# Starting SBUF tiles at multiples of 512 bytes in a hybrid decoder layer

## The chip, the cores and the metric

One core of a Trainium2 chip runs the whole layer in one launch. The metric is device microseconds of one execution; the kernel before takes 1169.69 us, the median of 3 runs (1168.28 to 1171.7).

## What is computed

One layer of a decoder on x of 512 tokens by 1024, in float32. Cut to what matters:

```python
x = x + 0.5 * swiglu(rms_norm(x), w_gate, w_up, w_down)          # D_FF = 2816
h = rms_norm(x); z, xbc, dt, q, k, v = split(h @ w_in)
xs, b, c = split(silu(causal_dwconv(xbc)))
y = rms_norm(ssd_chunked(xs, softplus(dt), -exp(a_log), b, c) * silu(z))   # 16 heads, chunks of 128
o = rms_norm(diff_attention(rms_norm(q), rms_norm(k), v))                  # 8 heads, causal
x = x + concat[y, o] @ w_out
x = x + 0.5 * swiglu(rms_norm(x), w_gate2, w_up2, w_down2)
```

## The kernel before

`hymba_layer` keeps activations transposed, as 8 blocks of 128 channels by 512 tokens. Matrix products are done in three float32r passes: an operand is split into a high part `hi` (rounded to float32r) and the rest `lo`, and hi·hi, hi·lo and lo·hi are summed in PSUM. `mm3` (lines 153 to 157) is that triple for a 128x128 block of weights (`lhsT`, the stationary operand, loaded by an LDWEIGHTS of its own for each matmul) and 512 columns of activations (`rhs`, the moving operand):

```python
PE.matmul(ps, lhsT=hi, rhs=xh, start=start, stop=False)
PE.matmul(ps, lhsT=hi, rhs=xl, start=False, stop=False)
PE.matmul(ps, lhsT=lo, rhs=xh, start=False, stop=stop)
```

Weights stream from HBM into `raw` (three buffers, SP's queue, line 106), ACT casts them to `whi` (line 113) and DVE subtracts to get `wlo` (line 114), four buffers each, pieces ahead of their use.

The stages in order:

- FFN1. Its first 6 blocks of D_FF go the plain way: `gu` (`std`, line 359, through `mm3`), 8 blocks of 3 matmuls for each of gate and up, with `xh`, `xl` moving. The other 16 go pair by pair through a seven-product scheme (`seven`, line 314): `product` (lines 307 to 312) runs matmuls of 256 columns with slices of `ah`, `al` moving, into `s`. The down product `dn` (`down`, line 339, through `mm3`) has `h` moving, and line 346 adds it to `x`.
- The mixer's projections: `xbc` (12 blocks, through `mm3`, `xhm` and `xlm` moving, line 565), dt, then z and v (`tok_pair`, lines 619 to 621), where a 128x128 block of `xhm` or `xlm` is stationary and 512 columns of `whi` or `wlo` move, in two pieces of 256; and q and k (`tok_proj`, lines 596 to 598), with 256 columns of weights moving. SSD (from line 645) runs between the z and v pieces, attention (`att_s`, `att_t`, `att_av`, `att_o`) between the q and k pieces. SSD and attention use float32 matmuls, which the trace shows as two records each.
- `wo` (`y_part`, `o_part`, lines 917 to 930, through `mm3`), with `yh`, `yl` or `ov`, `ool` moving.
- FFN2, as FFN1, but with 4 plain blocks and 18 in pairs; its `xh`, `xl` come from the pool `x2` on the right side of SBUF.

Tiles come from pools that lie one behind the other in SBUF, and a tile's start in its partition is the sum of what lies before it. `const` comes first, then `wpool` (raw, whi, wlo), `tiny`, `xn` (`xh`, `xl`), and on top of these the pools of a stage; `x1` and `x2` grow from the other end (`side="right"`). A tile whose size is no multiple of 512 shifts all behind it: `const` holds small ones, `row` is 1456 float32 wide (line 412), `u` 515 (line 455).

Of the kernel before, what the change touches and what calls it, by code (L numbers as in the profile page):

```python
# [8 lines left out]
F32 = mybir.dt.float32  # L9
# [9 lines left out]
P = 128  # L19
T = 512  # L20
# [14 lines left out]
NROW = 1456  # L35
# [3 lines left out]
def hymba_layer(ctx: ExitStack, tc: tile.TileContext, xT, gu1, dn1, wxbc, wdt, wz, wv, wqk,  # L39
# [3 lines left out]

    const = ctx.enter_context(tc.tile_pool(name="const", bufs=1))
    wpool = ctx.enter_context(tc.tile_pool(name="wpool", bufs=4))
    dram = ctx.enter_context(tc.tile_pool(name="dram", bufs=1, space=DRAM))
    pspool = ctx.enter_context(tc.tile_pool(name="psum", bufs=8, space=PSUM))

# [137 lines left out]
    G.memset(epst, EPS)  # L186

    tiny = ctx.enter_context(tc.tile_pool(name="tiny", bufs=2))
    xn_cm = tc.tile_pool(name="xn", bufs=1)
    xnpool = xn_cm.__enter__()  # L190

# [217 lines left out]

    mix_cm = tc.tile_pool(name="mix", bufs=1)  # L410
    mix = mix_cm.__enter__()
    row = mix.tile([P, NROW], F32, name="row")
    nc.sync.dma_start(row, rows.partition_broadcast(P))
    vt = [mix.tile([P, NB, 256], F32, tag=f"v{g}", name=f"v{g}") for g in range(4)]

# [21 lines left out]
    ssd = ssd_cm.__enter__()  # L437
# [7 lines left out]
    ea = ssd.tile([P, NB, 16], F32, name="ea")  # L445
    dsd = ssd.tile([P, NB, 16], F32, name="dsd")
    cdec = ssd.tile([P, NB, 16], F32, name="cdec")
    acs_d = dram.tile([64, P], F32, name="acs_d")
    ysave = dram.tile([P, KD, NB, P], F32, name="ysave")

    cv_cm = tc.tile_pool(name="conv", bufs=2)
    cv = cv_cm.__enter__()

    def conv_tile(t, ps):
        u = cv.tile([P, T + 3], F32, tag="u", name="u")
        G.memset(u[:, 0:3], 0.0)
        V.tensor_mul(u[:, 3:], ps, nm.rbc)
        a = cv.tile([P, T], F32, tag="a", name="a")

        def cw(i):  # L460
            c = C_CW + t * 4 + i
            return col[:, c:c + 1]

        V.tensor_scalar(a, u[:, 3:], cw(3), col[:, C_CB + t:C_CB + t + 1], op0=ALU.mult, op1=ALU.add)
        for i in range(3):
            V.scalar_tensor_tensor(a, u[:, i:i + T], cw(i), a, op0=ALU.mult, op1=ALU.add)
        if t >= 8:
            dst = (bT if t < 10 else cT)[:, t % 2, :]
        else:
            dst = cv.tile([P, T], F32, tag="xst", name="xst")  # L470
        S.activation(dst, a, AF.Silu)
        return dst
# [75 lines left out]
    for n, pair in enumerate(order):  # L548
        if n == 2:
            pt_dt = dt_proj()  # L550
            small_consts()
        ps = [pP(f"xbc{n}{i}") for i in range(2)]
        if n == 0:
            ws = [piece(), piece()]
            for k in range(KD):
                for p_, w in zip(ps, ws):
                    mm3(p_, w, k, nm.xh[:, k, :], nm.xl[:, k, :], k == 0, k == KD - 1)
            fin = nm.finish()
            next(fin)
            first_ps = ps  # L560
            continue
        for i in range(2):
            w = piece()
            for k in range(KD):
                mm3(ps[i], w, k, nm.xh[:, k, :], nm.xl[:, k, :], k == 0, k == KD - 1)
            if n == 1 and i == 0:
                next(fin)
                pend0 = [(t, conv_tile(t, p_)) for t, p_ in zip(order[0], first_ps)]
        if n == 3:
            dt_finish(pt_dt)  # L570
        for t, dst in pend:
            conv_tr(t, dst)
        pend = [(t, conv_tile(t, ps[i])) for i, t in enumerate(pair)]
        if n == 1:
            pend = pend0 + pend
# [517 lines left out]
```

## Time and profile before

| | |
|---|---|
| median of 3 runs | 1169.69 us |
| the profiled execution, its own time | 1168.65 us |
| its span, first to last instruction | 1166.9 us |
| mean granted TensorE clock | 0.997 of 2.4 GHz |
| PE busy | 1158.3 us |
| DVE busy | 854.2 us |
| ACT busy | 543.5 us |
| DMA, mean rate | 102 GB/s |

PE's matmuls overlap each other in the trace: a matmul's record runs from its start to its modelled end, and the next starts before. The distance between the starts of two neighbours, called a step below, is read from the timeline.

### The profile page before, as it was taken

Reading aid. Unit: us, or ns where it says so; the run is one execution under the profiler, and the core shown is the slowest. Engines: PE = TensorE matmul, PEld = TensorE weight load, DVE = VectorE, ACT = ScalarE, POOL = GpSimd, SP = SyncE. Lnnn points to the kernel's source line nnn. Section 1 sums busy time; section 2 is a strip of 40 time slices with the busy share of each in tenths; the row PEclk is TensorE's granted clock in tenths of the full one; section 3 lists DMA queues with packets and bytes.
Section 4 is the critical chain, followed back from the end, with each engine's and each line's share of the span. In section 5 each row is a group of like instructions: output and inputs, shape, how many; then the busy total and the mean of one; then the engine's idle time right before and its main releaser. Section 6 shows DMA issues by size and latency. Waiting matters only on the chain.

```text
span 1166.9 us, 17871 instructions
## 1 busy us (share of the span) xinstructions
PE 1158.3 (99%) x7051; PEld 1004.0 (86%) x7051; DVE 854.2 (73%) x1501; ACT 543.5 (47%) x922; POOL 36.1 (3%) x63
## 2 busy tenths in 40 slices
PE   8999999999999999999999999999999999999998
PEld 6789999999887788788988887688889999999986
DVE  7877877877768975785477877435798888777763
ACT  5533343434345459784466656334354443334331
POOL 1000000000013000000000000022000000000000
PEclk9999999999999999999999999899999999999999
DMA  7223333433246242333321105054223333333332
GB/s 238 88 73 96 91 111 103 110 98 105 86 123 213 73 145 86 114 100 100 109 73 44 67 19 154 19 171 127 69 67 99 110 114 95 117 97 99 113 96 86
DMA packets 44692, 119.49 MB, mean 102 GB/s; under 512 B 4864, under 2 KB 10176, under 8 KB 44608
## 3 DMA queue, kind: packets, MB, share of 16 engines
q1 hardware_dynamic: 43328, 114.15, 32.3%
q0 software_dynamic: 1280, 4.20, 1.0%
q8 instruction: 55, 0.90, 0.3%
q14 instruction: 29, 0.24, 0.1%
HBM read 112.00 MB, written 6.32 MB: 101 GB/s over the span
## 4 chain that ended last, share of the span: by engine, by line
PE 99%; DVE 0%; DMA 0%; SPq 0%; ACT 0%; issue 0%
PE s L312 10%; PE s L310 10%; PE s L311 10%; PE dn L157 7%; PE dn L156 7%; PE dn L155 7%; PE gu L155 3%; PE gu L157 3%; PE gu L156 3%; PE qk L596 3%; PE wo L155 3%; PE wo L156 3%; PE wo L157 3%; PE qk L598 3%; PE qk L597 3%; PE sc L835 2%
## 5 line engine op out<-in xcount | busy, mean ns | idle before, releaser
L113 ACT CAST whi<-raw 128x1024 fp32r<-128x1024 f32 (+2 forms) x217 | 189.4, 875 | 312.8 <-PE s L311 124.1
L114 DVE TENSOR_TENSOR wlo<-raw,whi 128x1024 fp32r<-128x1024 f32 (+3 forms) x225 | 223.0, 993 | 129.2 <-ACT whi L113 122.1
L311 PE MATMUL s<-al,whi 128*128 128x256 f32 x952 | 266.4, 281 | 0.0
L310 PE MATMUL s<-ah,whi 128*128 128x256 f32 x952 | 265.4, 281 | 0.0
L312 PE MATMUL s<-ah,wlo 128*128 128x256 f32 x952 | 264.9, 281 | 0.0
L311 PEld LDWEIGHTS s<-al,whi 128*128 128x128 f32 x952 | 179.4, 188 | 2.2
L310 PEld LDWEIGHTS s<-ah,whi 128*128 128x128 f32 x952 | 178.8, 188 | 2.3
L312 PEld LDWEIGHTS s<-ah,wlo 128*128 128x128 f32 x952 | 178.3, 188 | 0.1
L156 PE MATMUL dn<-h,whi 128*128 128x512 f32 x352 | 139.0, 395 | 0.0
L157 PE MATMUL dn<-h,wlo 128*128 128x512 f32 x352 | 138.7, 395 | 0.0
L155 PE MATMUL dn<-h,whi 128*128 128x512 f32 x352 | 137.9, 395 | 0.0
L113 ACT CAST whi<-tw 128x1024 fp32r<-128x1024 f32 x68 | 70.3, 1050 | 143.0 <-PE s L311 68.9
L114 DVE TENSOR_TENSOR wlo<-tw,whi 128x1024 fp32r<-128x1024 f32 x68 | 81.9, 1218 | 2.9 <-ACT whi L113 2.9
L157 PEld LDWEIGHTS dn<-h,wlo 128*128 128x128 f32 x352 | 66.1, 188 | 15.0
L155 PEld LDWEIGHTS dn<-h,whi 128*128 128x128 f32 x352 | 66.0, 188 | 14.3
L156 PEld LDWEIGHTS dn<-h,whi 128*128 128x128 f32 x352 | 66.1, 188 | 13.9
L596 PE MATMUL qk<-whi,xhm 128*128 128x256 f32 x256 | 74.3, 290 | 0.0
L598 PE MATMUL qk<-whi,xlm 128*128 128x256 f32 x256 | 71.9, 281 | 0.0
L597 PE MATMUL qk<-wlo,xhm 128*128 128x256 f32 x256 | 71.5, 279 | 0.0
L346 DVE SCALAR_TENSOR_TENSOR x<-dn,x 128x512 f32<-128x512 f32 x64 | 44.0, 687 | 37.3 <-PE dn L157 36.7
L155 PE MATMUL gu<-xh,whi 128*128 128x512 f32 x160 | 64.2, 402 | 1.8 <-DVE acc L232 1.7
L157 PE MATMUL gu<-xh,wlo 128*128 128x512 f32 x160 | 62.9, 393 | 0.0
(274 smaller groups left out, 2101.2 us busy)
## 6 DMA issues: line engine op xcount, KB each, us to landing
raw<-in_gu SPq DMA_DIRECT2D x86, 512.0 KB, 3.7
raw<-in_dn SPq DMA_DIRECT2D x48, 384.0 KB, 3.2
raw<-in_wqk SPq DMA_DIRECT2D x16, 512.0 KB, 3.7
raw<-in_wxbc SPq DMA_DIRECT2D x12, 512.0 KB, 3.7
raw<-in_wo SPq DMA_DIRECT2D x10, 512.0 KB, 3.7
raw<-in_dn SPq DMA_DIRECT2D x16, 256.0 KB, 2.7
raw<-in_wz SPq DMA_DIRECT2D x16, 256.0 KB, 3.0
ab<-acs_d SPq DMA_DIRECT2D x8, 512.0 KB, 4.0
```

What stands on the lines that cost most here:

```text
L113: S.copy(hi[:, a:b], raw[:, a:b])
L114: V.tensor_sub(lo[:, a:b], raw[:, a:b], hi[:, a:b].bitcast(F32))
L155: PE.matmul(ps, lhsT=hi, rhs=xh, start=start, stop=False)
L156: PE.matmul(ps, lhsT=hi, rhs=xl, start=False, stop=False)
L157: PE.matmul(ps, lhsT=lo, rhs=xh, start=False, stop=stop)
L310: PE.matmul(ps, lhsT=hi, rhs=ah[:, i, a], start=i == 0, stop=False)
L311: PE.matmul(ps, lhsT=hi, rhs=al[:, i, a], start=False, stop=False)
L312: PE.matmul(ps, lhsT=lo, rhs=ah[:, i, a], start=False, stop=i == 3)
L346: V.scalar_tensor_tensor(x[d], ps, 0.5, x[d], op0=ALU.mult, op1=ALU.add)
L596: PE.matmul(o, lhsT=xh, rhs=hi, start=k == 0, stop=False)
L597: PE.matmul(o, lhsT=xh, rhs=lo, start=False, stop=False)
L598: PE.matmul(o, lhsT=xl, rhs=hi, start=False, stop=k == KD - 1)
```

## The change

It sets unused tiles and wider tiles between the others. `padc` adds 288 bytes to `const`, `padr` 480 to the right side, `padt` 32 to `tiny`, `pads` 192 to `ssd`; `row` grows from 5824 to 6144 bytes and `u` from 2060 to 2560, both used to their old width.

```diff
     wpool = ctx.enter_context(tc.tile_pool(name="wpool", bufs=4))
+    const.tile([P, 72], F32, name="padc")
+    rpad = ctx.enter_context(tc.tile_pool(name="rpad", bufs=1, side="right"))
+    rpad.tile([P, 120], F32, name="padr")
...
     tiny = ctx.enter_context(tc.tile_pool(name="tiny", bufs=2))
+    tiny.tile([P, 8], F32, tag="padt", name="padt", bufs=1)
...
-    row = mix.tile([P, NROW], F32, name="row")
+    row = mix.tile([P, 1536], F32, name="row")[:, :NROW]
...
     cdec = ssd.tile([P, NB, 16], F32, name="cdec")
+    ssd.tile([P, 48], F32, name="pads")
...
-        u = cv.tile([P, T + 3], F32, tag="u", name="u")
+        u = cv.tile([P, T + 128], F32, tag="u", name="u")[:, :T + 3]
```

z and v are projected onto 512 columns in both kernels. Each engine's instructions, their order and their waits are the same in both programs. What differs is where the tiles start; the two compiled programs place them so, in bytes past a multiple of 512 (every buffer of a name is alike):

| tile | before | after |
|---|---|---|
| `raw`, `whi`, `wlo` | 224 | 0 |
| `xh`, `xl` of FFN1, `xhm`, `xlm`, `yh`, `yl` | 192 | 0 |
| `ah`, `al`, `h`, `tx` | 192 | 0 |
| `x` (`x1`, `x2`), `xh`, `xl` of FFN2 | 480 | 0 |
| v, `ov`, `ool`, `qT`, `kT`, `pe`, `aT`, `on`, `xs`, `sz`, `bT`, `cT` | 384 | 0 |
| `ab`, `xdt`, `y` | 192 | 0 |
| `state` | 128 | 448 |
| `ident`, `identr` | 480 | 256 |
| `acc`, `rbc` | 0 | 288 |

FFN2's `xh` and `xl` take bytes 194528 to 227295 of a partition before; FFN1's `h` buffers reach from 131776 to 205503, and those that `dn` reads from 93.03 to 95.59 us start at 189120 and 197312.

## Rows read from the trace of the kernel before

**Rows 1.** The page: busy time, and the chain that ended last by engine.

```profile
PE 1158.3 (99%) x7051; PEld 1004.0 (86%) x7051; DVE 854.2 (73%) x1501; ACT 543.5 (47%) x922; POOL 36.1 (3%) x63
...
PE 99%; DVE 0%; DMA 0%; SPq 0%; ACT 0%; issue 0%
```

**Rows 2.** Busy time by stage; then PEclk, DMA share, GB/s.

```profile
core 0: us, PE busy (x) PEld busy (x) DVE busy (x) ACT busy (x) POOL busy (x), PEclk, DMA share, GB/s
...
78.00:345.00 267.00, 267.00 (x1807) 246.01 (x1806) 203.52 (x315) 102.04 (x127) 0.00 (x0) 1.00 0.35 102
...
700.00:745.00 45.00, 43.79 (x209) 30.97 (x209) 29.68 (x75) 25.41 (x60) 0.00 (x0) 0.92 0.33 100
...
860.00:1167.00 307.00, 303.26 (x2046) 278.81 (x2044) 231.54 (x352) 113.87 (x138) 0.00 (x0) 1.00 0.34 101
```

**Rows 3.** Groups of PE: count | busy us, mean ns of a record | idle before.

```profile
L310 PE MATMUL s<-ah,whi 128*128 128x256 f32 x952 | 265.4, 281 | 0.0
...
L155 PE MATMUL dn<-h,whi 128*128 128x512 f32 x352 | 137.9, 395 | 0.0
L596 PE MATMUL qk<-whi,xhm 128*128 128x256 f32 x256 | 74.3, 290 | 0.0
...
L157 PE MATMUL gu<-xh,wlo 128*128 128x512 f32 x160 | 62.9, 393 | 0.0
...
L156 PE MATMUL xbc<-xlm,whi 128*128 128x512 f32 x96 | 38.0, 395 | 0.0
...
L619 PE MATMUL z<-whi,xhm 128*128 128x512 f32 x64 | 27.1, 423 | 0.0
L155 PE MATMUL wo<-yh,whi 128*128 128x512 f32 x64 | 26.5, 414 | 0.0
...
L859 PE MATMUL at<-ident,pe 128*128 128x128 f32 x80 | 13.8, 272 | 1.2 <-DVE nmx L842 1.2
```

**Rows 4.** Timeline, FFN1's `gu`, first and last of 66: start us, length us.

```profile
44.82 0.40 PE L156 MATMUL gu<-xl,whi 128*128 128x512 f32 x1
...
59.99 0.40 PE L155 MATMUL gu<-xh,whi 128*128 128x512 f32 x1
```

**Rows 5.** Timeline, FFN2's `gu`, first and last of 68.

```profile
834.73 0.39 PE L156 MATMUL gu<-xl,whi 128*128 128x512 f32 x1
...
849.92 0.39 PE L157 MATMUL gu<-xh,wlo 128*128 128x512 f32 x1
```

**Rows 6.** Timeline, FFN1's `dn`, first and last of 12.

```profile
93.03 0.40 PE L155 MATMUL dn<-h,whi 128*128 128x512 f32 x1
...
95.59 0.40 PE L157 MATMUL dn<-h,wlo 128*128 128x512 f32 x1
```

**Rows 7.** Timeline, z, first and last of 10.

```profile
449.62 0.40 PE L621 MATMUL z<-whi,xlm 128*128 128x512 f32 x1
...
451.72 0.39 PE L621 MATMUL z<-whi,xlm 128*128 128x512 f32 x1
```

**Rows 8.** Timeline, `wo` from `ov` and `ool`, first and last of 44.

```profile
781.72 0.39 PE L157 MATMUL wo<-ov,wlo 128*128 128x512 f32 x1
...
791.79 0.40 PE L155 MATMUL wo<-ov,whi 128*128 128x512 f32 x1
```

**Rows 9.** Timeline, FFN2's `s`, first and last of 103.

```profile
871.84 0.28 PE L310 MATMUL s<-ah,whi 128*128 128x256 f32 x1
...
883.91 0.28 PE L312 MATMUL s<-ah,wlo 128*128 128x256 f32 x1
```

**Rows 10.** Timeline, `qk`, first and last of 105.

```profile
561.75 0.28 PE L596 MATMUL qk<-whi,xhm 128*128 128x256 f32 x1
...
573.89 0.28 PE L598 MATMUL qk<-whi,xlm 128*128 128x256 f32 x1
```

**Rows 11.** The chain in order of time: start us, us; two float32 passes of 512 columns.

```profile
467.36 0.86 PE pd L690 x2
```

**Rows 12.** Groups of DVE from 0 to 345 us.

```profile
L346 DVE SCALAR_TENSOR_TENSOR x<-dn,x 128x512 f32<-128x512 f32 x25 | 17.2, 689 | 11.8 <-PE dn L157 11.5
...
L137 DVE TENSOR_TENSOR tw<-raw 128x512 f32<-128x512 f32 x16 | 11.1, 692 | 10.1 <-DMA raw<-in_gu 10.0
```

## The prediction, made before the changed kernel ran

> **What bounds the kernel now.** I began with the page's busy shares and the chain that ended last: PE is busy 99% of the span and holds 99% of the chain [rows 1]. By stage [rows 2], PE is busy in every microsecond of the first feed-forward layer's main part (267.00 of 267.00) and nearly so elsewhere, at a granted clock of 1.00, while DVE, the next engine, is busy 203.52 of those 267 us. So the span is a sum of PE steps, and the question is how long a step is. "Busy" can't tell: the record of a 512-column matmul lasts 395 ns [rows 3], but the next one starts long before it ends. What counts is the step, the distance between the starts of neighbours, and for this I took from the timeline the first and the last row of an unbroken run and the number of matmuls in it.
>
> FFN1's `gu` matmuls (512 float32r columns): 66 of them start from 44.82 to 59.99 us, 65 steps in 15.17 us, 233.4 ns each [rows 4]. FFN2's `gu`, the same code, shapes, weight buffers and order: 68 from 834.73 to 849.92, 67 steps, **226.7 ns** [rows 5]. Both at clock 1.00; at 2.4 GHz, the level this is, 512 columns at one a cycle are 213.3 ns, so one carries an excess of 20.1 ns, the other of 13.4. I know one difference between them: where the moving operand starts. By the table of starts it lies 192 bytes past a multiple of 512 in FFN1 and 480 in FFN2; the weights are at 224 in both.
>
> Other rows fit a dependence on the start. `dn` reads `h` at 192 and steps by 233 ns even where `h` lies in the region that FFN2's `xh` takes later (93.03 to 95.59, eleven steps, 232.7 [rows 6]), so the region isn't it. z, whose moving operand is the weight tile at 224 and whose stationary one is at 192, makes nine steps in 2.10 us, 233.3 [rows 7]; `wo` with `ov` at 384 makes 43 in 10.07, 234.2 [rows 8]. With 256 columns, `s` (192) makes 102 steps in 12.07 us, 118.3 [rows 9], and `qk` (224) 104 in 12.14, 116.7 [rows 10], against 106.7 at one column a cycle. A float32 pass, which takes two cycles a column, shows next to no excess: two of 512 columns in 0.86 us [rows 11], 430 ns against 426.7. So what depends on the start is float32r's full-rate reading of SBUF. Every long run in this trace but one has its two operands at unlike places modulo 64 (192 and 224, 384 and 224), and the exception, 480 and 224, is the fast one. (I leave out the sixteen matmuls of the dt projection, alike too, since they load 48 or 16 columns of weights.)
>
> **The change, part by part.** No instruction is added, removed or moved: each engine's order, with its waits, is the same. The padding costs no time of its own, since the pad tiles are never written, and `row`'s and `u`'s wider tiles are used to their old width. What changes is the starts: weights, `xh`, `xl`, `ah`, `al`, `h`, `ov`, `ool` and the attention's tiles all begin at a multiple of 512.
>
> *512 columns.* There are 352 x 3 of `dn`, 160 x 3 of `gu`, 96 x 3 of `xbc`, 64 x 6 of `wo` and 64 x 6 of z and v [rows 3]: 2592. Of these, FFN2's 192 `gu` (4 pairs x 8 blocks x 3) are already at 226.7. No row shows a start at 0. The bounds: below, no excess but the 3 ns that the float32 pass shows (216.6); above, the sign turned round (third rival). I take 226.7, because 480 is nearest to 0 in both readings I can make of it: 32 bytes short of a multiple of 512, and both operands alike modulo 64, as they will be everywhere. 2400 x 6.7 ns = **16.1 us**.
>
> *256 columns, `s`.* 952 x 3 = 2856 [rows 3]. No fast row exists, so I scale the excess as the 512-column rows do: 13.4/20.1 = 0.667 of 11.6 is 7.7, a step of 114.4, 3.9 saved: **11.1 us**. Counting multiples of 512 crossed inside the operand instead (four to three for 512 columns, 5.0 each; two to one for 256, 5.8 each) gives 12.0 for the first term and 16.6 for this, the same sum within 2 us.
>
> *256 columns, `qk`.* 768 x 3.3 ns (10.0 to 6.7) = **2.5 us**.
>
> Together 29.7 us. What could withhold it is a wait on another engine. In both feed-forward layers DVE's load of 76% would become 78%, and PE, busy 267.00 of 267.00, never waits for it there now [rows 2]. Between 437 and 745 us PE does wait for DVE now and then (1.2 us idle at the softmax's `nmx` [rows 3], 43.79 of 45.00 busy in one stage [rows 2]), and z, v, `qk` and part of `wo`, about 6 us of the gain, lie there; I leave out 1.7 us of that, a little over a quarter: **28 us**.
>
> *DVE, ACT, DMA.* In FFN1 a DVE instruction of 128x512 takes 689 ns with `x` at 480 and 692 with `tw` and `raw` at 192 and 224 [rows 12], so I price their new starts at nothing; PE covers a few ns of theirs in any case, and the DMA queues are 0.35 busy in the stages that count [rows 2].
>
> A rule speaks against all this. The Trainium skill, "SBUF — State Buffer", section "Operand start alignment", asks only that a start be a multiple of the element's size, calls that a rule of legality and not of speed, and says under "Who interferes with whom" that PE never waits on anyone; "TensorE: Matmul & The Clock Gate", "Back-to-back issue gap", gives one gap for 512 columns, 215.7 ns, whatever the address. By these pages the change would do nothing; the trace's 233.4 and 226.7 side by side disagree with them.
>
> **The sum.** The profiled execution took 1168.65 us (span 1166.9), 1.0 under the median of 1169.69. 1168.65 - 28 = 1140.6, and with the 1.0 put back **1141.7 us** against the median.
>
> **Rivals.**
> 1. *The excess goes altogether.* In FFN2's `gu` only the moving operand was near a multiple of 512, the weights were at 224; if their start carries the rest, both aligned would leave the 3 ns of [rows 11]: 2400 x 16.8 + 192 x 10.1 + 2856 x 8.3 + 768 x 6.7 = 71 us, hence 1099; half of that rest gone is 1120. For it: that weights matter can't be excluded, since all runs have them at 224 or 192. Against: no float32r run comes near 216.6.
> 2. *Nothing changes.* Either something else than the start separates the two `gu` runs, or FFN2's 226.7 is a matter of the exact pair 480 and 224, 256 bytes apart, and a pair at distance 0 behaves as the pairs 32 apart do. Then 1170 (plus 1.3 if FFN2's `gu` falls back to 233.4). For it: one fast pair is thin evidence. Against: at distances 32 and 160 the steps are 233.4 and 234.2, so distance doesn't order them. The skill's two pages named above would have this rival.
> 3. *Slower.* PE reads the moving operand and, underneath, the next weights, one load for each matmul [rows 1]. Put at the same place modulo 512, the two reads could meet at each line and hold each other up. The place is every float32r matmul; the price, for want of a row, is what the start has been seen to make, with the other sign: +6.7, +3.9 and +3.3 ns, and for FFN2's `gu` +13.4: 30 + 2.6 us, hence 1202, half as much 1186. It decides once an aligned step is over 233.4. Against it: the one pair alike modulo 64 is the fastest.
> That the padding doesn't do what it says is excluded for the operands of these matmuls by the table of starts; `state`, `ident`, `acc` and `rbc` stay off multiples of 512, but they are read by float32 passes, which show no excess.
>
> **How the numbers follow.** The forecast (1156 with half the gain lost, 1127 if the weights' start brings a third of what the first rival has beyond it, 71 - 28 = 43 us) has 0.63; the first rival 0.14, the second 0.12, the third 0.11. A measurement of this kernel tells about 0.3%, 3.5 us, from no change. Faster: 0.63 + 0.14 = 0.77; same 0.12; slower 0.11. The range takes in the forecast, the second rival and the nearer part of the first: 1105 to 1172, about 0.83.
>
> **What would show it.** In the profile of the changed kernel, with as many instructions as before: runs of `dn`, `xbc`, `wo`, z and v stepping by about 227 ns and their records 6 to 7 ns shorter than 395; `s` at 114 to 115 and `qk` at 113 to 114; FFN2's `gu` unchanged near 227. PE should still be 99% busy, the feed-forward stages about 2.5 to 3% shorter, and DVE's busy time the same. FFN2's `gu` falling to 217 with the rest speaks for the first rival; `dn` still at 233 for the second; steps above 234 for the third. If steps shorten but the span doesn't, the waits of PE on DVE and ACT must have grown by as much. The prediction is wrong if 512 aligned columns don't step within some 3 ns of 227.

## The result, and the profile after

| | before | after |
|---|---|---|
| median | 1169.45 us, 8 runs (1166.98 to 1171.86) | 1163.33 us, 8 runs (1162.02 to 1165.63) |
| the profiled execution, its own time | 1168.65 us | 1165.11 us |
| its span | 1166.9 us | 1163.4 us |

The ratio is 0.995, with a 95% interval from 0.9935 to 0.9964: the change takes 6.1 us off. That is faster, as forecast, but the forecast was 28 us. It lies inside the range only because the range was stretched up to 1172 for the second rival; the forecast with half its gain lost was 1156. So the question is where the other 22 us are.

The page of the kernel after: busy time, the chain by engine, and the PE groups that answer to [rows 1, 3].

```profile
PE 1154.1 (99%) x7051; PEld 1011.4 (87%) x7051; DVE 854.2 (73%) x1501; ACT 543.4 (47%) x922; POOL 36.9 (3%) x63
...
PE 99%; DMA 0%; DVE 0%; SPq 0%; POOL 0%; issue 0%; ACT 0%
...
L314 PE MATMUL s<-ah,whi 128*128 128x256 f32 x952 | 267.1, 283 | 0.0
...
L158 PE MATMUL dn<-h,whi 128*128 128x512 f32 x352 | 136.2, 390 | 0.0
...
L601 PE MATMUL qk<-whi,xhm 128*128 128x256 f32 x256 | 75.0, 293 | 0.0
...
L159 PE MATMUL gu<-xl,whi 128*128 128x512 f32 x160 | 63.5, 397 | 0.0
```

PE still holds 99% of the span and of the chain, and DVE and ACT are busy for as long as before. So nothing took PE's place, and no wait swallowed a gain. What moved is the length of the matmuls, in both directions: a record of `dn` is shorter (395 to 390 ns), one of `s` longer (281 to 283), one of `qk` longer (290 to 293).

The windows of the same three stages as in [rows 2] say it too (busy time by engine, then PEclk, DMA share, GB/s):

```profile
core 0: us, PE busy (x) PEld busy (x) DVE busy (x) ACT busy (x) POOL busy (x), PEclk, DMA share, GB/s
...
78.00:345.00 267.00, 267.00 (x1810) 248.36 (x1809) 203.53 (x314) 102.14 (x126) 0.00 (x0) 1.00 0.35 102
...
700.00:745.00 45.00, 43.80 (x207) 30.93 (x207) 29.34 (x74) 25.58 (x58) 0.00 (x0) 0.92 0.31 100
...
860.00:1163.00 303.00, 299.75 (x2032) 278.54 (x2030) 229.86 (x351) 113.83 (x138) 0.00 (x0) 1.00 0.34 101
```

From 78 to 345 us PE is busy in every microsecond, as before, and starts 1810 matmuls where it started 1807. The forecast had the feed-forward stages 2.5 to 3% shorter, which would be some 50 matmuls more here.

The steps, from the timeline of the kernel after: FFN1's `gu` (67 matmuls from the first row to the second), `qk` (102), FFN2's `s` (102), FFN2's `dn` (68).

```profile
44.82 0.39 PE L159 MATMUL gu<-xl,whi 128*128 128x512 f32 x1
...
59.78 0.39 PE L159 MATMUL gu<-xl,whi 128*128 128x512 f32 x1
...
559.78 0.28 PE L603 MATMUL qk<-whi,xlm 128*128 128x256 f32 x1
...
571.90 0.28 PE L602 MATMUL qk<-wlo,xhm 128*128 128x256 f32 x1
...
867.77 0.28 PE L315 MATMUL s<-al,whi 128*128 128x256 f32 x1
...
879.89 0.28 PE L316 MATMUL s<-ah,wlo 128*128 128x256 f32 x1
...
1129.67 0.39 PE L158 MATMUL dn<-h,whi 128*128 128x512 f32 x1
...
1144.86 0.39 PE L159 MATMUL dn<-h,whi 128*128 128x512 f32 x1
```

`gu`: 14.96 us over 66 steps, **226.7 ns**, where it was 233.4 [rows 4]: to the tenth the value that FFN2's `gu` had before [rows 5]. `dn`: 15.19 over 67, 226.7. But `s`: 12.12 over 101, **120.0 ns**, where it was 118.3 [rows 9], and `qk` 12.12 over 101, 120.0, where it was 116.7 [rows 10]. The 512-column steps became shorter by what was forecast; the 256-column steps became longer.

Summed over all neighbours in each group of the two traces (each step counted up to 45 ns over one column a cycle, so that waits stay out), beside the terms of the forecast:

| group, matmuls | before, us | after, us | change | forecast |
|---|---|---|---|---|
| `gu` FFN1, 288 | 67.3 | 66.0 | -1.3 | -1.9 |
| `dn`, 1056 | 245.8 | 240.5 | -5.3 | -7.1 |
| `xbc`, 288 | | | -1.6 | -1.9 |
| `wo`, 384 | 90.2 | 88.0 | -2.2 | -2.6 |
| z and v, 384 | | | -1.3 | -2.6 |
| all of 512 columns but FFN2's `gu` | | | **-11.8** | -16.1 |
| `s`, 2856 | 338.3 | 342.3 | **+4.1** | -11.1 |
| `qk`, 768 | 91.3 | 93.2 | **+1.9** | -2.5 |

That is -5.8 us of steps (from sums before rounding), and the medians differ by 6.1. The gain is the balance of two opposite effects, of which the forecast had one. The profiled execution itself is only 3.5 us shorter. Near its start it shows a stretch that the profiled execution of before lacks (windows of the kernel after, PE alone; then PEclk, DMA share, GB/s):

```profile
core 0: us, PE busy (x), PEclk, DMA share, GB/s
...
8.00:9.00 1.00, 0.00 (x0) 0.76 1.05 392
9.00:10.20 1.20, 1.06 (x3) 0.50 1.06 387
...
14.00:15.00 1.00, 1.00 (x4) 0.50 0.05 20
15.00:16.00 1.00, 1.00 (x6) 0.83 0.50 90
```

From about 8.5 to 15.3 us the granted clock is 0.50, the lower of the two levels. It falls while PE is idle, from 6.8 to 9.1 us; the profiled execution of before is idle there for 1.7 us instead of 2.4, and keeps 1.00. It costs FFN1's first `gu` about 3 us. Three of the eight executions of after have a mean clock of 0.994 and the others 0.996 or 0.997, and it turns up in some executions of other kernels below, so the medians, not the two profiles, give the change's price.

### The profile page after: what moved, and what is told of

The parts are those of the page before. It is cut to its first block, busy times and chain, and to the rows that moved or that the text cites. A ratio compares the mean times of both kernels' runs of the same rounds, so it can differ in the third digit from the quotient of the medians.

```text
span 1163.4 us, 17871 instructions
## 1 busy us (share of the span) xinstructions
PE 1154.1 (99%) x7051; PEld 1011.4 (87%) x7051; DVE 854.2 (73%) x1501; ACT 543.4 (47%) x922; POOL 36.9 (3%) x63
## 4 chain that ended last, share of the span: by engine, by line
PE 99%; DMA 0%; DVE 0%; SPq 0%; POOL 0%; issue 0%; ACT 0%
PE s L316 10%; PE s L315 10%; PE s L314 10%; PE dn L159 7%; PE dn L158 7%; PE dn L160 7%; PE gu L158 3%; PE gu L159 3%; PE gu L160 3%; PE qk L601 3%; PE qk L603 3%; PE qk L602 3%; PE wo L158 3%; PE wo L159 3%; PE wo L160 3%; PE sc L840 2%
## 5 line engine op out<-in xcount | busy, mean ns | idle before, releaser
L315 PEld LDWEIGHTS s<-al,whi 128*128 128x128 f32 x952 | 182.6, 192 | 1.9
L314 PEld LDWEIGHTS s<-ah,whi 128*128 128x128 f32 x952 | 181.9, 192 | 2.0
L316 PEld LDWEIGHTS s<-ah,wlo 128*128 128x128 f32 x952 | 181.5, 192 | 0.1
L159 PE MATMUL dn<-h,whi 128*128 128x512 f32 x352 | 137.4, 391 | 0.0
L158 PE MATMUL dn<-h,whi 128*128 128x512 f32 x352 | 136.2, 390 | 0.0
L159 PE MATMUL gu<-xl,whi 128*128 128x512 f32 x160 | 63.5, 397 | 0.0
```

The source lines that it names most:

```text
L314: PE.matmul(ps, lhsT=hi, rhs=ah[:, i, a], start=i == 0, stop=False)
L315: PE.matmul(ps, lhsT=hi, rhs=al[:, i, a], start=False, stop=False)
L316: PE.matmul(ps, lhsT=lo, rhs=ah[:, i, a], start=False, stop=i == 3)
```

## The experiments

The theory that they test, called P: *a float32r step depends on how far the moving operand's start lies from the start of the weights that are loaded underneath, modulo 256 bytes; multiples of 512 as such do nothing.* It fits the 512-column steps of both traces: FFN2's `gu` before (480 and 224, distance 256) and the long runs of after (distance 0) step by 226.7, all other pairs of before by 233 to 234.

**A map by starts.** A kernel with nothing but float32r matmuls, each group of 24 with the weights at one of 16 starts and the moving operand at one of 16, 32 bytes apart:

```diff
+    for n in (512, 256):
+        for m in range(16):
+            for w in range(16):
+                ps = psum.tile([P, T], F32, tag="P", name=f"p{n}")[:, :n]
+                for k in range(KD):
+                    hi, lo = (z[:, w * 8 + k * P:w * 8 + k * P + P] for z in (wh, wl))
+                    mh, ml = (z[:, m * 8 + k * n:m * 8 + k * n + n] for z in (xh, xl))
+                    PE.matmul(ps, lhsT=hi, rhs=mh, start=k == 0, stop=False)
+                    PE.matmul(ps, lhsT=hi, rhs=ml, start=False, stop=False)
+                    PE.matmul(ps, lhsT=lo, rhs=mh, start=False, stop=k == KD - 1)
```

> This kernel computes nothing of the layer: it runs groups of 24 float32r matmuls in the kernel's triple (hi and xh, hi and xl, lo and xh, one weight load each), 256 groups with 512 columns and 256 with 256, one for each pair of starts of the moving and the stationary operand, both 0 to 480 bytes past a multiple of 512 in steps of 32, with no other engine at work; x is written out unchanged. Theory P (what counts is the place of the moving operand relative to the weights that are read meanwhile): the step depends on the difference of the two starts. Difference 0 or 256: 227 ns with 512 columns and 120 with 256, the same 13.3 ns over one column a cycle, a fixed price for each weight load; difference 32 either way: 233 and 117 to 118. Theory M (the moving operand's start alone, the price counted by lines or blocks crossed): the step is the same for all 16 weight starts at one moving start, 227 at 0 and 480, 233 at 192 and 224. Theory W (the weights' start): the same for all moving starts. If no group is near 227 and 233, the kernel's steps hang on the other engines at work, and none of the three holds.

Measured: with 512 columns the steps order by distance alone, and repeat every 256 bytes; the starts themselves do not show (the pairs of one distance lie within 2 ns, but for the kernel's very first group). With 256 columns most pairs do the same, and some stand out: 116.9 to 117.9 at distance 32, 117.3 to 120.1 at 160, 114.0 to 118.0 at 192. Medians in ns over the 32 pairs of each distance, a pair's step being the mean of its group:

| moving start less weights' start, modulo 256 | 0 | 32 | 64 | 96 | 128 | 160 | 192 | 224 |
|---|---|---|---|---|---|---|---|---|
| 512 columns | 226.7 | 233.4 | 229.3 | 233.4 | 233.5 | 233.9 | 233.4 | 233.1 |
| 256 columns | 119.6 | 117.9 | 117.8 | 120.1 | 118.4 | 117.3 | 117.8 | 118.3 |

Three groups in the map's timeline: 512 columns with the moving operand at 192 and the weights at 224 (23 matmuls), the same at 480 and 224 (23), 256 columns at 128 and 128 (24).

```profile
593.49 0.39 PE L48 MATMUL p<-xh,wh 128*128 128x512 f32 x1
...
598.62 0.40 PE L49 MATMUL p<-xl,wh 128*128 128x512 f32 x1
...
1395.60 0.39 PE L48 MATMUL p<-xh,wh 128*128 128x512 f32 x1
...
1400.59 0.39 PE L49 MATMUL p<-xl,wh 128*128 128x512 f32 x1
...
1638.78 0.28 PE L48 MATMUL p<-xh,wh 128*128 128x256 f32 x1
...
1641.54 0.28 PE L50 MATMUL p<-xh,wl 128*128 128x256 f32 x1
```

5.13 us over 22 steps is 233.2, 4.99 over 22 is 226.8, 2.76 over 23 is 120.0. These are the values of FFN1 before, FFN2 before and `s` after, with no other engine at work: DVE, ACT and the DMAs have no part in them. The two widths are in conflict at distance 0: the best for 512 columns, next to the worst for 256. (Four of the pairs at distance 192 gave 114 with 256 columns; more on that below.)

**The weights alone 32 bytes further.** All other tiles stay at multiples of 512.

```diff
-    const.tile([P, 72], F32, name="padc")
+    const.tile([P, 80], F32, name="padc")
...
-    tiny.tile([P, 8], F32, tag="padt", name="padt", bufs=1)
```

> The changed kernel with raw, whi and wlo 32 bytes further on and all else where it is (tiles of one pool move, two pads are resized). Theory P: every pair of operands is 32 apart again, as in most of the kernel before, so dn, gu, xbc and wo step by 233 ns and s and qk by 117 to 118, FFN2's gu too (233), and the time is that of the kernel before or 1 us over: 1168 to 1172. Theory M: dn, gu, xbc, wo and s stay at 227 and 120; only z, v and qk, whose moving operand is a weight tile, could change: 1160 to 1166. Theory W: all float32r steps change alike.

Measured: 1169.43 us, ratio 1.0004 (0.999 to 1.0019): the whole gain is gone. Its timeline, FFN2's `gu` (66 matmuls) and FFN2's `s` (104):

```profile
834.78 0.40 PE L159 MATMUL gu<-xl,whi 128*128 128x512 f32 x1
...
849.95 0.40 PE L158 MATMUL gu<-xh,whi 128*128 128x512 f32 x1
...
870.80 0.28 PE L315 MATMUL s<-ah,wlo 128*128 128x256 f32 x1
...
882.98 0.28 PE L315 MATMUL s<-ah,wlo 128*128 128x256 f32 x1
```

233.4 and 118.3: with `xh` still at 0 modulo 512, FFN2's `gu` is as slow as FFN1's was before. The distance is 224 modulo 256, as in before's FFN1 (192 less 224), and both values are the ones before had there. A start at a multiple of 512 is worth nothing by itself; what P says of these steps holds.

**All tiles 32 bytes further, and the weights 256 further.** The other side of the same test: in the first none of the moved operands and weights starts at a multiple of 512, in the second none of the weights, and all distances stay 0 modulo 256. The first:

```diff
-    const.tile([P, 72], F32, name="padc")
+    const.tile([P, 80], F32, name="padc")
...
-    rpad.tile([P, 120], F32, name="padr")
+    rpad.tile([P, 112], F32, name="padr")
```

> The changed kernel with every tile 32 bytes further on (const padded by 32 bytes more, the right side by 32 less), so that nothing starts at a multiple of 512 but all operands are as far from each other as in the changed kernel. Theory P: the same steps (dn 227, s 119.9, qk 119.7) and time as the changed kernel, 1163. If multiples of 512 matter by themselves: dn 233, as in the kernel before, 1169 or more.

The second:

```diff
-    const.tile([P, 72], F32, name="padc")
+    const.tile([P, 136], F32, name="padc")
...
-    tiny.tile([P, 8], F32, tag="padt", name="padt", bufs=1)
+    tiny.tile([P, 72], F32, tag="padt", name="padt", bufs=1)
```

> The changed kernel with raw, whi and wlo 256 bytes further on, all else where it is. The first map's step repeats every 256 bytes of distance, so by theory P nothing changes: dn 227, s 119.9, 1163. If the distance counts modulo 512, a distance of 256 is another one, and the steps differ from the changed kernel's.

Measured: 1162.15 us, ratio 0.9942 (0.9921 to 0.9962), and 1165.38 us, 0.9952 (0.9935 to 0.9968), beside after's 0.995 (0.9935 to 0.9964). Both have after's steps: `dn` 228.0, `s` 119.9 and `qk` 119.7 in the mean. FFN1's `gu` in the kernel with the weights at 256 (68 matmuls):

```profile
44.77 0.39 PE L159 MATMUL gu<-xl,whi 128*128 128x512 f32 x1
...
59.96 0.39 PE L160 MATMUL gu<-xh,wlo 128*128 128x512 f32 x1
```

15.19 us over 67 steps: 226.7. So what the change does, it does by making distances 0 modulo 256.

**Distances chosen by width.** If P holds, the 512-column matmuls should stay at distance 0 and `s` be taken away from it. A pad ahead of `ah` and one behind `al` do that in both FFNs and leave `h` where it was. For 160, the map's best for 256 columns:

```diff
         sp, hp = sp_cm.__enter__(), hp_cm.__enter__()
+        sp.tile([P, 40], F32, name=f"pa{name}")
         ah = sp.tile([P, 4, 7, 256], F32R, name=f"ah{name}")
         al = sp.tile([P, 4, 7, 256], F32R, name=f"al{name}")
+        sp.tile([P, 88], F32, name=f"pb{name}")
```

> The changed kernel with ah and al 160 bytes further on (a pad ahead of them and one behind, so that nothing else moves); weights, xh, h, ov stay at 0. Theory P with the first map: the 2856 matmuls of s step by 117.3 ns instead of 119.9, all others as in the changed kernel (dn, gu 227, qk 120), so 2856 x 2.6 ns = 7.4 us less than the changed kernel: 1155.9, ratio to the kernel before about 0.988. A theory by which all operands must be aligned for the 512-column matmuls to be fast, or by which the start of s does not matter: 1163, or slower.

Measured: 1159.84 us, ratio 0.9921 (0.9906 to 0.9935). Better than after, by half of what P gave. FFN2's `s` (103 matmuls):

```profile
863.80 0.28 PE L316 MATMUL s<-ah,whi 128*128 128x256 f32 x1
...
875.91 0.28 PE L318 MATMUL s<-ah,wlo 128*128 128x256 f32 x1
```

12.11 us over 102 steps is 118.7, where the map's median is 117.3. P's direction holds with 256 columns, its values do not: the map's median misses by 1.4 ns, and its own pairs at this distance lie between 117.3 and 120.1.

**A second map: `xh`, `xl` and the low weights at starts of their own.** The loop of the first map, with the high weights at 0, `xh` at a, `xl` at b and `wl` at c, each from 0 to 224 in steps of 32:

```diff
+    for n in (256, 512):
+        for a in range(8):
+            for b in range(8):
+                for c in range(8):
+                    group(n, a, b, c)
```

> Computes nothing of the layer: as the first map, but the starts of xh, xl and wl are set apart (each 0 to 224 in steps of 32, wh at 0), 512 groups with 256 columns and 512 with 512. Theory P says that each step depends on one difference alone, that of the operand moving and of the weights loaded under it: in a triple these are three differences, and the mean step of a group is the mean of three entries of the first map (between 117.3 and 120.1 with 256 columns, 226.7 at the least with 512). A theory by which a step depends on what came before it would show groups well below 117.3 with 256 columns (the first map has cells at 114.0), or 512-column groups under 226.7.

Measured: with 512 columns no group is under 228.4. With 256 columns the best is `xh` and `xl` at 64, weights at 0; in the timeline of this kernel, 24 matmuls of that group, and then the 24 that the first map has with the same starts (moving operand at 64, weights at 0):

```profile
427.99 0.28 PE L46 MATMUL p<-xh,wh 128*128 128x256 f32 x1
...
430.60 0.28 PE L48 MATMUL p<-xh,wl 128*128 128x256 f32 x1
```

```profile
1536.49 0.28 PE L48 MATMUL p<-xh,wh 128*128 128x256 f32 x1
...
1539.20 0.28 PE L50 MATMUL p<-xh,wl 128*128 128x256 f32 x1
```

2.61 us over 23 steps is 113.5, 2.71 over 23 is 117.8. Every matmul of both has the distance 64, from the same starts. So with 256 columns one distance has more than one steady step, and which one a group falls into depends on something else, perhaps on what ran before it. The first map points that way: its 256-column groups that stand out from their distance by over half a nanosecond all lie among the first ten of the 16 groups that share a moving start, and the same ones stand out 256 bytes further on. A mean of the three single entries does not tell a mixed group's step at either width (correlation about 0.1 with 256 and with 512 columns; with 512 the groups reach from 228.4 to 236.7, the first map's entries from 226.7 to 233.9). So P, which gives each single matmul its step by its own distance, fails here. What the runs support is narrower: where all matmuls of a triple have one distance, as in the layer's groups of 512 columns, the step with 512 columns goes by it. Whether the kernel could reach 113 was the question for the next four.

**`ah`, `al` at 224, 64, 192 and 32.** The same two pads, of 56 and 72, 16 and 112, 48 and 80, 8 and 120 elements:

```diff
+        sp.tile([P, 16], F32, name=f"pa{name}")
...
+        sp.tile([P, 112], F32, name=f"pb{name}")
```

> The changed kernel with ah and al alone put back to their distance of before from the weights (224 modulo 256, that is 32 short), all else at 0. If the loss in the changed kernel is the step of s, s goes back from 119.9 to 118.4 ns: 2856 x 1.5 = 4.3 us less than the changed kernel, 1159.0, ratio to the kernel before 0.991. If the loss lies elsewhere (a wait, another engine): 1163.

> The changed kernel with ah and al 64 bytes on. Theory P (the distance alone sets the step): s at 117.8 ns as in the first map, 2856 x 2.1 = 6.0 us less than the changed kernel, 1157.3. Theory R (at one distance there are several steady steps, and what ran just before decides which one holds): s may run at the 113.3 that the second map showed for all three operands at 64, 2856 x 6.6 = 18.8 us less, 1144.5, or at a mixture.

> The changed kernel with ah and al 192 bytes on. Theory P: s at 117.8 ns, 1157.3. Theory R: s may run at the 114.0 of two cells of the first map, 2856 x 5.9 = 16.9 us less than the changed kernel, 1146.5.

> The changed kernel with ah and al 32 bytes on. Theory P: s at 117.9 ns, 1157.6. Theory R: the maps show 116.7 to 118.3 at this distance, so 1154 to 1159.

Measured, beside the kernels above (distance of `s`; steps in ns, means of their group):

| kernel | `s` distance | `s` | `dn` | median, us | ratio |
|---|---|---|---|---|---|
| after | 0 | 119.9 | 228.0 | 1163.33 | 0.995 (0.9935 to 0.9964) |
| `ah`, `al` at 160 | 160 | 118.7 | 227.2 | 1159.84 | 0.9921 (0.9906 to 0.9935) |
| at 224 | 224 | 118.3 | 228.2 | 1158.78 | 0.9899 (0.9876 to 0.9921) |
| at 64 | 64 | 117.8 | 228.3 | 1156.97 | 0.9891 (0.9872 to 0.991) |
| at 32 | 32 | 116.7 | 227.8 | 1155.99 | 0.9874 (0.9855 to 0.9892) |
| at 192 | 192 | 117.8 | 226.8 | 1155.28 | 0.9868 (0.9849 to 0.9887) |

FFN2's `s` at 64 (104 matmuls):

```profile
862.83 0.28 PE L316 MATMUL s<-ah,whi 128*128 128x256 f32 x1
...
874.96 0.28 PE L316 MATMUL s<-ah,whi 128*128 128x256 f32 x1
```

at 192 (104):

```profile
861.80 0.28 PE L317 MATMUL s<-al,whi 128*128 128x256 f32 x1
...
873.93 0.28 PE L317 MATMUL s<-al,whi 128*128 128x256 f32 x1
```

and at 32 (106):

```profile
863.72 0.28 PE L316 MATMUL s<-ah,whi 128*128 128x256 f32 x1
...
875.97 0.28 PE L318 MATMUL s<-ah,wlo 128*128 128x256 f32 x1
```

12.13 us over 103 steps at 64 and at 192, 117.8; 12.25 over 105 at 32, 116.7. The 113 of the second map does not come in the kernel. At 32 `s` runs at the 116.7 that `qk` had before at the same distance [rows 10], not at the 117.9 of most of the first map's pairs. Undoing the change for `s` alone (224, the distance it had before) gives 1158.78: that is after less 4.6 us, and shows that `s` is where the change lost. At 192 and at 32 both kernels are beaten, by 14 to 15 us against before; the two can't be told apart.

**What in the two reads makes the step.** A map of weight columns (128, 64, 32, 16) against moving columns (512 to 128), weights at 0 and the moving operand at 0 to 224; then the same in bfloat16 and in float32:

```diff
+    for cols in (128, 64, 32, 16):
+        for n in (512, 384, 256, 128):
+            for d in range(8):
+                ps = psum.tile([P, T], F32, tag="P", name=f"c{cols}n{n}")[:cols, :n]
+                for k in range(KD):
+                    hi, lo = (z[:, k * P:k * P + cols] for z in (wh, wl))
+                    mh, ml = (z[:, d * 8 + k * n:d * 8 + k * n + n] for z in (xh, xl))
```

> Computes nothing of the layer: groups of 24 float32r matmuls with 128, 64, 32 and 16 columns of weights and 512, 384, 256 and 128 moving columns, the moving operand 0 to 224 bytes from the weights, then bfloat16 and float32 groups at the same distances. If the excess over one column a cycle is the price of the weight load underneath, it shrinks with the weight columns: 13.3 ns at 128 columns and distance 0 becomes 6 to 7 at 64 and 3 at 16, whatever the moving columns are. If it is the price of the moving operand's own lines, it stays 13.3 for 16 weight columns and grows with the moving columns. Bfloat16 and float32, which read half the bytes in a cycle: at most 3 ns over one column a cycle (one in two cycles), the same at all distances.

Measured, in ns, lowest and highest over the eight distances (for 512 moving and 128 weight columns the distance 0 is left out: its group ran first in the kernel, with most steps at 427):

| moving columns | 128 weight columns | 64 weight columns | 16 weight columns |
|---|---|---|---|
| 512 | 229.3 to 234 | 226.6 to 231.5 | 231.0 to 232.1 |
| 256 | 113.7 to 119.6 | 113.3 to 119.0 | 113.7 to 117.7 |
| 128 | 109.4 to 111.8 | 60 | 60 |

A moving operand of 384 columns has an order of its own: 173.3 to 173.5 at the distances 0, 32 and 64, 176.2 to 176.7 at 96 to 160 (128 weight columns). bfloat16 steps by 215.9 and 109.2 (512 and 256 columns) and a float32 pass by 429.2 and 215.9, at every distance. Three groups of the timeline: 128 moving columns with 128 weight columns (23 matmuls) and with 64 (24), and 512 with 16 (24).

```profile
126.73 0.27 PE L55 MATMUL c128n<-xh,wh 128*128 128x128 f32 x1
...
129.18 0.28 PE L56 MATMUL c128n<-xl,wh 128*128 128x128 f32 x1
...
244.25 0.22 PE L55 MATMUL c64n<-xh,wh 128*64 128x128 f32 x1
...
245.63 0.22 PE L57 MATMUL c64n<-xh,wl 128*64 128x128 f32 x1
...
371.43 0.39 PE L55 MATMUL c16n<-xh,wh 128*16 128x512 f32 x1
...
376.74 0.39 PE L57 MATMUL c16n<-xh,wl 128*16 128x512 f32 x1
```

2.45 us over 22 steps is 111.4; with half the weight columns it is 60.0 (1.38 over 23). So a full float32r weight load seems to take about 110 ns, and to set the step when the stream is shorter. With 16 weight columns the step of 512 columns is 230.9 (5.31 over 23) and, over all distances, hardly moves. That speaks for a distance that acts through the weight load. With 256 columns it can't be said: there the step still spreads over 4 ns with 16 weight columns, in another order of the distances. And 230.9 is *more* than the 226.7 that a full load at distance 0 has in the first map and in the layer. The load doesn't just add to a stream that would be at one column a cycle without it; the stream has an excess of its own of some 18 ns (231 less 213.3), and a full load at distance 0 lowers it. An account by a fixed price for each weight load (13.3 ns at distance 0 with both widths: 226.7 less 213.3, 119.9 less 106.7), which would have explained the miss neatly, fell with this run.

## Why the prediction was wrong

**What held.** PE's steps are the bound, and no other engine came in: the 1.7 us withheld for waits on DVE does not show as a loss. DVE's, ACT's and the DMA's costs of nothing held. FFN2's `gu` stayed at 226.7. The size that I took for an aligned 512-column step, 226.7, was right to the tenth. The reasons for it were not: 480 was taken as near a multiple of 512, and both operands as alike modulo 64. The distances 64, 128 and 192 are alike modulo 64 too, and step by 229.3 to 233.5 in the first map. The number came out because 480 and 224 happen to lie 256 apart. (The count of 192 for FFN2's `gu` is right; the product given for it lacks the factor 2 of gate and up.)

**Where the first term lost.** 11.8 of 16.1 us came. Part is the half-clock stretch in `gu`. The rest is mostly that a step needs time to settle. `dn` takes several matmuls after a run of `s`, which is 1.3 ns a step in its mean, 1.4 us in all; a stretch of the timeline after, first the last `s`:

```profile
882.05 0.28 PE L316 MATMUL s<-ah,wlo 128*128 128x256 f32 x1
882.17 0.40 PE L158 MATMUL dn<-h,whi 128*128 128x512 f32 x1
...
883.56 0.39 PE L158 MATMUL dn<-h,whi 128*128 128x512 f32 x1
883.79 0.39 PE L159 MATMUL dn<-h,whi 128*128 128x512 f32 x1
```

From 882.17 to 883.56 are six steps, 231.7 ns each. The starts are printed to 0.01 us; the finer ones of the trace give the first six steps of another such run as 234, 235, 229, 232, 231 and 227 ns, then 226 to 227. With `ah`, `al` at 192 this settling is absent and `dn` is at 226.8 in the mean. z and v, which are broken up by float32 matmuls, settle anew after each break, over six to ten steps, and have 229.7 in the mean, 1.1 us in all. Where z runs on for longer it reaches the same 226.7 (28 matmuls, 27 steps in 6.12 us):

```profile
448.13 0.39 PE L626 MATMUL z<-whi,xlm 128*128 128x512 f32 x1
...
454.25 0.39 PE L626 MATMUL z<-whi,xlm 128*128 128x512 f32 x1
```

**The step that failed.** "*256 columns, `s`.* ... No fast row exists, so I scale the excess as the 512-column rows do", 118.3 to 114.4 and 11.1 us, and the same for `qk`, 2.5 us. Measured, in means: 118.4 to 119.9 and +4.1 us, 117.0 to 119.7 and +1.9. These two terms are off by 19.6 us, most of the 22 that are missing. The working behind them took the start for the cause and the width for a mere size. What the runs showed instead: the cause is the distance between the moving operand and the weights, and the best distance at one width is among the worst at the other. There was evidence for this in the rows: `s` (distance 224) and `qk` (distance 32) were 1.6 ns apart at 256 columns, while the 512-column rows at the same two distances, `gu` and z, were 0.1 apart. So the two widths did not scale with each other in the trace of before. I read past it, and gave the second term no bound of its own on the side of a loss.

**The rivals.** The first fell: no 512-column float32r group with 128 weight columns, in any run, is under 226.6. The second had the right account of FFN2's `gu`, "a matter of the exact pair 480 and 224, 256 bytes apart", but with the wrong end: a pair at distance 0 behaves as the pair at 256 does, which is a period of 256. Its argument against itself, that distance doesn't order the steps since 32 and 160 are alike, held only because both lie on the slow side. The third rival had the sign at 256 columns (+1.4 and +2.6 ns where it priced +3.9 and +3.3); with 512 columns the sign is the opposite. Its mechanism, that the moving read and the weight load hold each other up at the same place, is not shown: a distance of 96 is as slow as 0 in the first map (120.1 and 119.6). It was treated as one mechanism for both widths, just as the forecast was.

**The pages.** That a start has nothing to do with speed was weighed as a rule against the change. The Trainium skill, "TensorE: Matmul & The Clock Gate", section "Step-by-step: what each phase is for", says that loading the next tile's weights takes no SBUF read bandwidth from the running matmul. The runs here don't bear that out for float32r: 32 bytes between the two operands move a step of 512 columns from 226.7 to 233.4, with no other engine at work in the first map. The 215.7 ns that the prediction takes from the section "Back-to-back issue gap" of the same page of the Trainium skill stands under other headings of it; that section gives about 216 for a matmul by itself and about 131 for a stream with weight loads. No run here comes near 131 with 512 columns; the bfloat16 groups of the third map, with their weight loads, step by 215.9.

**What stays open.** What in SBUF or in PE's reading repeats every 256 bytes; why a full weight load at distance 0 leaves a 512-column stream shorter than hardly any load does; what decides between the steady steps at one distance (113.5 or 117.8 at 64); and what sets the step where a triple mixes distances. That it is the matmuls just before was not tried by itself. Whether the distance counts from the weights loaded underneath or from a matmul's own is not told apart either, since both have the same start modulo 256 in every group but the mixed ones. The moving starts were tried in multiples of 32 bytes only.

## What to carry to other kernels

For float32r, a change of placement is priced by the distance between the two operands of each matmul, separately for each width, from steps between starts in the timeline, never from a record's mean length. Don't carry an effect from one width to another: for these float32r matmuls the distance 0 modulo 256 is best with 512 columns and bad with 256, and a placement that leaves the 512-column groups at 0 and takes `s` to 32 or 192 is worth 14 to 15 us where one rule for all tiles is worth 6. Where no row shows the sign of an effect, its term needs a bound on each side of zero, however neat the scaling.

## What the runs showed of the hardware that was not expected

- With 512 columns, and one distance in the whole triple, a float32r step depends on the distance of moving operand and weights modulo 256 bytes, and not on either start: 226.7 ns at 0, 229.3 at 64, 233 to 234 at the other multiples of 32. With 256 columns most pairs lie between 117 and 120, with 0 and 96 the slowest.
- bfloat16 (215.9 ns) and float32 passes (429.2) of 512 columns show no such dependence.
- Several steady steps exist at one distance with 256 columns: 113.5 and 117.8 at 64, 114 and 117.8 at 192. After a break or a change of width six to ten matmuls can pass before the step is steady.
- A full float32r weight load is not free: with 128 moving columns it sets the step, 111.4 ns against 60.0 with half the weight columns or fewer.
- The clock falls to the lower level for 3 to 7 us near the start in some executions and not in others; the mean clocks, 0.994 and 0.997, say that this happens with one and the same program.
